# A hybrid decoder step: the sample's recurrent states updated pair by pair, the head norms' roots in two batches, and the sample's gates ordered behind a later tile

## The chip, the cores and the metric

The kernel runs on one core of a Trainium2 chip. The core has a matrix engine (PE, with its weight loads shown apart as PEld), a vector engine (DVE), a scalar engine (ACT), a general engine (POOL) and SP, whose queue issues the DMA transfers here. Each engine works through its own queue of instructions strictly in order; engines wait for each other by semaphores. The metric is the device time of one execution in microseconds, the median of several runs.

## The reference: what is computed

One inference step of a single decoder layer, over 2048 prompt positions and over 64 sample rows (8 sequences of 8 new positions each). Every row is normalised and goes through one input projection; its columns are split between two mixers and their gates:

```python
h = rmsnorm(x, norm_w)
z = h @ w_in
q, k, v, qb, kb, vb, g_lr, gate_a, gate_b = jnp.split(z, split_points(), axis=-1)
...
o_a = attend(q, k, v)
log_a = jax.nn.log_sigmoid((g_lr @ w_gate_up + b_gate).astype(jnp.float32)) / GATE_TAU
o_b, s_fin = gla_chunked(heads(qb, H_B) * (DK_B ** -0.5), heads(kb, H_B), heads(vb, H_B),
                         heads(log_a, H_B), s0)
o_b = rmsnorm(o_b, gla_norm_w)
mixed = jnp.concatenate(
    [o_a.reshape(B, L, D_A) * jax.nn.silu(gate_a.astype(jnp.float32)),
     o_b.reshape(B, L, D_B) * jax.nn.silu(gate_b.astype(jnp.float32))], axis=-1)
y = x + mixed.astype(x.dtype) @ w_out
```

Mixer A is a dilated sliding-window attention with 8 heads, a mixture of three branches. Mixer B is a gated linear attention with 4 heads, key width 64 and value width 128. It carries a state per sequence and head; a chunk ends with

```python
state = (jnp.exp(b_last)[..., None] * state
         + jnp.einsum('bhsk,bhsv->bhkv', kc * jnp.exp(b_last[:, :, None] - b), vc))
```

The output of each head of mixer B is normalised by the root of its mean square. The new states of the 8 sample sequences are outputs of their own.

## The kernel before

The 2048 prompt rows are 16 tiles of 128 (`NT`), the sample is one tile of 64 rows (`"s"`). The kernel goes through these stages: the projections q, k, v with the first two branches of the attention; the projection `qkb` with the third branch; the projections `g` and `vb`, and then `gb`, beside the linear attention; and the output stage, in which every tile's gated mixture is multiplied with `w_out`, beside the sample's attention over the cached keys and values. Intermediate results go through DRAM (`ob_d` holds mixer B's outputs, `ga_d` and `gb_d` the gates' inputs).

**What sets the order.** Stages are Python generators. `weave` traces several of them in turns: each has a number of expected turns, and the one with the smallest share done goes next; one that yields `WAIT` is passed over. This fixes the program's order. The framework then plans each engine's queue at compile time: a planner (`schedule_with_timeline_sim=True`) goes through the program with modelled durations, and takes an instruction for an idle engine among those that it holds to be ready. Buffers of a pool are reused under a tag (`bufs` of them), and memory of a closed pool is reused tile by tile; an instruction that needs a buffer waits for the last user of what lay there. With `tc.issue_after(x)`, instructions on the engine of `x` are queued behind `x`, without a semaphore.

**The stage around the change.** The last `weave` of the linear attention runs the projection `gb` (`rest("gb")`, 130 turns; PE lines L1137, evicted by ACT at L752), the prompt's recurrence (`gla_prompt`, weight 32), the sample's part (`sample_gla`, weight 32) and the loading of `w_out` in two halves (`load_w`, scaled and converted at L659 on ACT and L660 on DVE). It ends when the recurrence and the sample's part have ended; what is left of `gb` then runs on beside `first_mixes`, which prepares tiles 0 and 1 for the output stage.

The recurrence goes through 8 blocks of 256 rows. `gla_core.front` computes a decay on POOL (L237), its exponential on ACT (L243) and two products on DVE (L248, L251); `back` multiplies on PE (L287). `chunk` finishes 128 rows: the state's sum on DVE (L1307), the output stored to `ob_d`, and in `gla_out` each head's sum of squares (L344), which goes into four columns of `ob_ss`, 4(t+1) for tile t and 0 for the sample.

`sample_gla` first builds its operands like a block of the recurrence, in a tile `own` that has the tag `vx`. Then, for both pairs of heads `p`, it multiplies queries with the old states (L1434, `O_s`), and squares the outputs. In a second loop over the pairs, halves `q` of the 8 sequences and heads `j` of the pair, POOL makes a block `vx` (L1460: the values masked to four sequences, 64x512), PE multiplies it with the keys (L1466, `U_s`), POOL decays the old states (L1471), and DVE adds (L1477). There is one `vx` buffer, so each block waits for the matmul of the block before; each pair's states are stored by SP at L1482. The generator yields 21 times in all, 14 of them in these two loops.

When all this has been traced, `rsqrt` turns all 68 columns of `ob_ss` into `ob_rs` at once: a scale and shift on DVE (L122), logarithm and exponential on ACT (L123, L125), a correction in three steps on DVE (L138 to L140).

**The output stage.** `combine(t)` loads the three attention branches (`oc`), computes the gates, loads mixer B's outputs (`obl`) and scales them by `ob_rs` on ACT (L1607), weighs the branches (L1694 to L1717, L1702 being the weights and L1710 and L1716 partly on POOL) and leaves the mixture as two 16-bit parts `mt` (`parts_of`: ACT L1616, DVE L1617). `gates(t)` clamps the gate inputs on DVE (L1586), takes exponential, logarithm and exponential on ACT (L1588, L1589, L1590), multiplies and takes maxima on DVE (L1592). `turned` transposes `mt` on PE (L1626, `tm`) and evicts it on ACT (L1627, `mh`); `finish` multiplies with `w_out` (L1668). `first_mixes` does `combine(0)` and `combine(1)` and, when `gb` is done, transposes tile 0. `prompt_out` then goes through the tiles, mixing two tiles ahead; at t = 8 it also traces the sample's `gates` and `normed`, which the planner may place as early as their inputs allow.

## Time and profile before

| | |
|---|---|
| median of 3 runs | 1339.93 us (1339.32 to 1349.03) |
| profiled execution | 1338.29 us, span 1336.5 us |
| mean granted TensorE clock | 0.977 |
| PE busy | 1215.3 us, 91% of the span |
| DVE, ACT, POOL busy | 899.3, 849.7, 615.6 us |
| last state sum of the sample (L1477) | starts at 1068.23 us |
| end of the `gb` projection on PE | 1077.84 us |
| first transposition of the output stage (L1626) | 1085.85 us |

All times inside an execution are counted from the start of the profiled span. "Idle before, releaser" tells how long an engine waited before an instruction and whose end released it; "issue" is a wait for which the profile shows no releaser. The granted clock is the share of full speed at which the matrix engine was let run in a stretch.

### The profile page before, as it was taken

How to read it: one execution, taken by the hardware profiler on the slowest of the kernel's cores; microseconds unless marked ns; L12 is line 12 of the kernel's file. 1: busy time of each engine (PE TensorE's matmuls, PEld its weight loads, DVE VectorE, ACT ScalarE, POOL GpSimd, SP SyncE). 2: the span in 40 equal slices, each digit the busy share in tenths (PEclk: the TensorE clock that was granted, in tenths of full speed). 3: DMA queues.
4: the chain of work that ended last, by engine and by line, in shares of the span. 5: the costliest groups of instructions: out<-in, count | busy, mean ns of one | idle time of the engine just before them, and what ended most of it. 6: DMA issues, size and time to landing. Idle time of an engine off the chain costs nothing.

```text
span 1336.5 us, 27968 instructions
## 1 busy us (share of the span) xinstructions
PE 1215.3 (91%) x9754; PEld 726.4 (54%) x9754; DVE 899.3 (67%) x2317; ACT 849.7 (64%) x2281; POOL 615.6 (46%) x596
## 2 busy tenths in 40 slices
PE   3897999989899798998999999999999969999998
PEld 1343565555556555576777666667555435444443
DVE  6366767787777876776763888776552368887751
ACT  5655787777668875878995565455662466555520
POOL 0076554778678735661112856665342133332310
PEclk9899999999999999999999989999999989999999
DMA  7859866777966599958886647453452777998952
GB/s 256 249 160 247 224 189 151 212 208 218 223 179 190 173 268 270 323 186 203 211 193 196 219 155 207 148 168 100 128 196 89 249 250 270 376 323 323 330 205 78
DMA packets 251807, 285.39 MB, mean 214 GB/s; under 512 B 125441, under 2 KB 160338, under 8 KB 251666
## 3 DMA queue, kind: packets, MB, share of 16 engines
q1 hardware_dynamic: 251666, 283.60, 71.0%
q8 instruction: 77, 1.26, 0.4%
q14 instruction: 64, 0.52, 0.1%
HBM read 183.12 MB, written 75.24 MB: 193 GB/s over the span
## 4 chain that ended last, share of the span: by engine, by line
PE 42%; DVE 17%; DMA 13%; issue 12%; POOL 9%; ACT 5%; SPq 2%; POOLq 0%; DVEq 0%; ACTq 0%
PE acc_gb L1137 5%; PE Y L1668 4%; PE acc_vb L1137 4%; PE acc_qkb L1137 4%; PE acc_q L1137 3%; PE acc_g L1137 3%; PE t L472 3%; PE s L454 3%; PE O L487 3%; PE acc_v L1137 2%; POOL pr L975 2%; PE acc_k L1137 2%; DMA T_q<-qp_d 2%; DVE ks L248 2%; DVE qs L251 2%
## 5 line engine op out<-in xcount | busy, mean ns | idle before, releaser
L1137 PEld LDWEIGHTS <-hr 128*128 128x128 f16 x1824 | 173.8, 99 | 127.7 <-issue 12.1
L1137 PEld LDWEIGHTS <-hl 128*128 128x128 f16 x1248 | 122.5, 100 | 154.4 <-issue 28.5
L465 ACT ACTIVATE p<-p,o 128x256 f32<-128x256 f32 (+1 forms) x384 | 173.4, 455 | 47.3 <-DVE o L462 40.6
L1668 PE MATMUL Y<-w_o,mh 128*128 128x512 f16 x768 | 179.3, 383 | 4.2 <-ACT mh L1627 3.5
L975 POOL TENSOR_TENSOR pr<-k,qb 128x512 f32<-128x512 f32 x96 | 132.9, 1384 | 90.1 <-DVE sck L980 54.9
L439 POOL TENSOR_TENSOR pt<-p,pt 128x512 f16<-128x512 f32 (+1 forms) x80 | 93.9, 1175 | 154.6 <-ACT pt L438 134.2
L487 PE MATMUL O<-v,pt 128*128 128x128 f16 x1200 | 111.6, 222 | 21.1 <-POOL pt L439 9.4
L1668 PEld LDWEIGHTS <-mh 128*128 128x128 f16 x768 | 72.3, 98 | 91.0 <-issue 10.9
L980 DVE TENSOR_REDUCE sck<-pr 128x8 f32<-128x512 f32 x128 | 85.7, 680 | 48.5 <-POOL pr L975 48.3
L472 PE MATMUL t<-ident,p 128*128 128x128 f32 x600 | 108.1, 283 | 9.1 <-ACT p L465 4.1
L487 PEld LDWEIGHTS <-pt 128*128 128x128 f16 x1200 | 82.6, 99 | 46.5 <-POOL pt L439 14.3
L1710 POOL TENSOR_TENSOR tc<-oc,w 128x512 f32<-128x512 f32 x32 | 44.2, 1401 | 134.6 <-DVE w L1702 96.4
L1137 PE MATMUL acc_v<-w_v,hl 128*128 128x512 f16 x384 | 97.0, 397 | 8.2 <-DVE vp L769 3.1
L1137 PE MATMUL acc_g<-w_g,hr 128*128 128x272 f16 (+1 forms) x768 | 102.5, 282 | 0.0
L462 DVE CUSTOM_DVE_ANT_0 p<-s,m3w,scl_s 128x128 f32<-128x128 f32 (+1 forms) x256 | 89.1, 395 | 14.6 <-PE s L454 7.2
L1137 PE MATMUL acc_q<-w_q,hl 128*128 128x512 f16 x384 | 91.4, 386 | 6.0 <-ACT zs_k L687 5.3
L1137 PE MATMUL acc_k<-w_k,hl 128*128 128x512 f16 x384 | 91.2, 383 | 3.0 <-ACT zs_k L687 2.5
L1137 PE MATMUL acc_vb<-w_vb,hr 128*128 128x512 f16 x384 | 92.0, 379 | 0.0
L454 PE MATMUL s<-kk,qq 128*128 128x256 f16 (+1 forms) x512 | 81.5, 270 | 8.2 <-DMA kk<-kp_d 4.5
L237 POOL TENSOR_TENSOR D_e<-b_e 128x512 f32<-128x512 f32 x56 | 61.0, 1094 | 58.5 <-ACT E L243 45.6
L1137 PE MATMUL acc_gb<-w_gb,hr 128*128 128x512 f16 x384 | 87.9, 380 | 0.0
L243 ACT ACTIVATE E<-D_e 128x256 f32<-128x256 f32 x112 | 43.7, 417 | 60.8 <-DVE ks L248 34.6
(507 smaller groups left out, 2595.9 us busy)
## 6 DMA issues: line engine op xcount, KB each, us to landing
k<-in_cache_k_win SPq DMA_DIRECT2D x104, 256.0 KB
sv<-in_cache_v_win SPq DMA_DIRECT2D x24, 1024.0 KB
hr<-h_d SPq DMA_DIRECT2D x44, 512.0 KB
qb<-q_d SPq DMA_DIRECT2D x64, 256.0 KB
o_d<-o SPq DMA_DIRECT2D x96, 132.0 KB
oc<-o_d SPq DMA_DIRECT2D x48, 264.0 KB
x<-in_x_prompt SPq DMA_DIRECT2D x16, 512.0 KB
h_d<-hl SPq DMA_DIRECT2D x16, 512.0 KB
```

What stands on the lines that cost most here:

```text
L237: dec = POOL.tensor_tensor(dv, bv, bv[:, :, 0:1, B - 1 : B].to_broadcast([P, M, 2, B]), ALU.subtract)
L439: POOL.tensor_tensor(l, f, h, ALU.subtract)
L454: PE.matmul(s_ps[:, i * w : (i + 1) * w], q, k, start=(n == 0), stop=(n == len(prods) - 1),)
L462: DVE.tensor_tensor_reduce(s[:, sl], s_ps[:, sl], mask, neg, BIG, ALU.add, ALU.min, nmf(i))
L465: ACT.activation(s[:, sl], s[:, sl], AF.Exp, bias=nmf(i), scale=-1.0, accum_out=denf(i))
L472: PE.transpose(p_ps[:, i * P : (i + 1) * P], t["s"][:, i * P : (i + 1) * P], ident[:])
L487: PE.matmul(o_, t["pt"][:, c, (i * nb + b) * P : (i * nb + b + 1) * P], vf(i, b), start=(n == 0), stop=(n == 2 * nb - 1),)
L975: POOL.tensor_tensor(pr[:], kt, qt, ALU.mult)
L980: DVE.tensor_reduce(out, pr[:].rearrange("p (u k d) -> p u k d", u=2, k=4), AX.X, ALU.add)
L1137: PE.matmul(z, a_[:, k, :], w[:, p_, k, cols], start=(k == 0 and i == 0), stop=(k == KT - 1 and i == 2),)
L1668: PE.matmul(Y[:], a_[:, k, :], w_[:, part, k, :512], start=(i == 0), stop=(i == len(prods) - 1),)
L1710: eng.tensor_tensor(t_[:], oc[:, g, :, 0:64], w[:, g].unsqueeze(2).to_broadcast([P, NH, HD]), ALU.mult,)
```

## The change

Four edits, in the stages from 950 us on.

1. **Pair by pair.** `sample_gla` has one loop over the pairs of heads. A pair's four blocks `vx` are traced first, into four buffers (`own` takes one of the four before); then the pair's outputs, the decays of its old states, a yield, and for each half the two matmuls and the sum. The generator yields 17 times, 10 of them in this loop.
2. **Roots in two batches, in place.** `ob_ss` now holds tile t in columns 4t and the sample in the last four. `head_scales` takes the roots of 32 columns, tiles 0 to 7, when chunk 9 has been traced, and of the other 36 after the recurrence. The roots overwrite the sums, and `normed` reads them from `ob_ss`.
3. **Marks.** `parts_of` keeps the two instructions that write a tile's `mt`.
4. **Sample's gates.** The sample's `gates` and `normed` are traced under `issue_after` of tile 2's marks: their ACT instructions are queued behind L1616 of tile 2, their DVE instructions behind L1617 of tile 2. Their DMA issues on SP aren't bound.

```diff
@@ -1238,6 +1238,7 @@
         )
         gpools = (gl, gt, ps_O, ps_S, ps_P)
 
+        gc_pool = gc
         masks = gc.tile([P, len(LEVELS), 32], F32, name="gmask")
         scan_m = gc.tile([P, 256], F32, name="scan_m")
         wgu = gc.tile([17, 256], F32, name="wgu")
@@ -1272,8 +1273,11 @@
         POOL.memset(ob_ss[:], 1.0)
 
         def at_heads(t):
-            c = 0 if t == "s" else 4 * (t + 1)
+            c = 4 * (NT if t == "s" else t)
             return ob_ss[:, c : c + 4]
+
+        def head_scales(pool, c):
+            rsqrt(pool, ob_ss[:, c], ob_ss[:, c], 1.0 / 128.0, P, c.stop - c.start, f"ob{c.start}")
 
         def chunk(core, gc):
             c, r0 = gc % 2, gc * P
@@ -1311,6 +1315,8 @@
                     )
             gla_out(gt, O, P, r0, f"c{gc}", at_heads(gc))
             mixed.add(gc)
+            if gc == 9:
+                head_scales(gc_pool, slice(0, 32))
 
         vbs = {}
 
@@ -1386,7 +1392,7 @@
             yield from upto("vb", "s")
             vb = g1.tile([NS, 512], F32, name="vb_s")
             SP.dma_start(vb[:], vb_d[S : S + NS, :])
-            own = g1.tile([P, 512], F32, name="own", tag="vx")
+            own = g1.tile([P, 512], F32, name="own", tag="vx", bufs=4)
             DVE.memset(own[:], 0.0)
             E, ks, qs = (
                 own[:, 0:128].rearrange("p (i c) -> p i c", i=2), own[:, 128:256], own[:, 256:320]
@@ -1419,7 +1425,22 @@
             qe, eb, kdt, Am = core.qe, core.eb, core.kdt, core.Ac
             so = A["state_gla_sample"][0]
             ebv = eb[:].rearrange("p a (b t) -> p a b t", t=8)
+            blocks = {}
+
+            def block(p, q, j):
+                h = 2 * p + j
+                vx = blocks[p, q, j] = g1.tile([NS, 4, P], F32, name=f"vx_{h}_{q}", tag="vx", bufs=4)
+                POOL.tensor_tensor(
+                    vx[:],
+                    vb[:, h * P : (h + 1) * P].unsqueeze(1).to_broadcast([NS, 4, P]),
+                    bm[:, 4 * q : 4 * q + 4].unsqueeze(2).to_broadcast([NS, 4, P]),
+                    ALU.mult,
+                )
+
             for p in range(2):
+                for q in range(2):
+                    for j in range(2):
+                        block(p, q, j)
                 O = ps_O.tile([P, 512], F32, name=f"O_s{p}", tag="O")
                 for j in range(2):
                     h, js = 2 * p + j, slice(64 * j, 64 * j + 64)
@@ -1449,31 +1470,21 @@
                         jk[:NS], ob[:, j * P : (j + 1) * P], AF.Square,
                         accum_out=at_heads("s")[:NS, h : h + 1],
                     )
+                for q in range(2):
+                    sq = S0[p][:, 4 * q : 4 * q + 4, :]
+                    POOL.tensor_tensor(
+                        sq, sq, ebv[:, p, 4 * q : 4 * q + 4, 7:8].to_broadcast([P, 4, P]), ALU.mult
+                    )
                 yield
-            for p in range(2):
                 for q in range(2):
                     sq = S0[p][:, 4 * q : 4 * q + 4, :]
                     U = ps_O.tile([P, 512], F32, name=f"U_s{p}{q}", tag="O")
                     for j in range(2):
                         h = 2 * p + j
-                        vx = g1.tile([NS, 4, P], F32, name=f"vx_{h}_{q}", tag="vx")
-                        POOL.tensor_tensor(
-                            vx[:],
-                            vb[:, h * P : (h + 1) * P].unsqueeze(1).to_broadcast([NS, 4, P]),
-                            bm[:, 4 * q : 4 * q + 4].unsqueeze(2).to_broadcast([NS, 4, P]),
-                            ALU.mult,
+                        PE.matmul(
+                            U[64 * j : 64 * j + 64], kdt[:NS, 0, 64 * h : 64 * h + 64],
+                            blocks.pop((p, q, j))[:], start=True, stop=True,
                         )
-                        PE.matmul(
-                            U[64 * j : 64 * j + 64], kdt[:NS, 0, 64 * h : 64 * h + 64], vx[:],
-                            start=True, stop=True,
-                        )
-                        if j == 0:
-                            POOL.tensor_tensor(
-                                sq, sq,
-                                ebv[:, p, 4 * q : 4 * q + 4, 7:8].to_broadcast([P, 4, P]),
-                                ALU.mult,
-                            )
-                            yield
                     DVE.tensor_tensor(
                         sq, sq, U[:].rearrange("p (b v) -> p b v", b=4), ALU.add
                     )
@@ -1564,8 +1575,7 @@
         va = cb1.tile([P, 2], F32, name="va")
         for i, c_ in enumerate((2048.0 / M_SCALE, 1.0 / (P_SCALE * W_SCALE * H_SCALE * V_SCALE))):
             DVE.tensor_scalar(va[:, i : i + 1], powers["v"][:], c_, None, ALU.mult)
-        ob_rs = cb1.tile([P, 4 * (NT + 1)], F32, name="ob_rs")
-        rsqrt(cb1, ob_rs[:], ob_ss[:], 1.0 / 128.0, P, 4 * (NT + 1), "ob")
+        head_scales(cb1, slice(32, 4 * (NT + 1)))
 
         def scales(c):
 
@@ -1601,20 +1611,24 @@
             pool, tag = (cb1, "obs") if t == "s" else (cb, "ob")
             ob = pool.tile([P, 512], F32, name=f"obl_{t}", tag=tag)
             SP.dma_start(ob[:n], ob_d[rows, :])
-            c = 0 if t == "s" else 4 * (t + 1)
+            rs = at_heads(t)
             for h in range(4):
                 s = slice(h * P, (h + 1) * P)
-                ACT.activation(ob[:n, s], ob[:n, s], AF.Copy, scale=ob_rs[:n, c + h : c + h + 1])
+                ACT.activation(ob[:n, s], ob[:n, s], AF.Copy, scale=rs[:n, h : h + 1])
             return ob
 
         ident16 = cb1.tile([P, P], F16, name="ident16")
         DVE.tensor_copy(ident16[:], ident[:])
 
+        marks = {}
+
         def parts_of(tag, mix):
 
             mt = cb.tile([P, 2, D], F16, name=f"mt_{tag}", tag="mt")
-            ACT.activation(mt[:, 0], mix[:], AF.Copy)
-            DVE.tensor_tensor(mt[:, 1], mix[:], mt[:, 0], ALU.subtract)
+            marks[tag] = (
+                ACT.activation(mt[:, 0], mix[:], AF.Copy).ins,
+                DVE.tensor_tensor(mt[:, 1], mix[:], mt[:, 0], ALU.subtract).ins,
+            )
             return mt
 
         def turned(tag, mt):
@@ -1750,7 +1764,10 @@
                 rows = slice(t * P, (t + 1) * P)
                 if t == NT // 2:
                     at_s = slice(S, S + NS)
-                    mixes["s"] = gates("s", NS, at_s), normed("s", NS, at_s)
+                    with ExitStack() as order:
+                        for m_ in marks[2]:
+                            order.enter_context(tc.issue_after(m_))
+                        mixes["s"] = gates("s", NS, at_s), normed("s", NS, at_s)
                 if t == NT - 1:
                     while "attended" not in mixed:
                         yield WAIT
```

## The prediction

> **What bounds the kernel now.** I read the page's busy times first, then busy time by stretches of the span, then the waits around the one stretch that stands out, and last that stretch instruction by instruction.
>
> ```profile
> PE 1215.3 (91%) x9754; PEld 726.4 (54%) x9754; DVE 899.3 (67%) x2317; ACT 849.7 (64%) x2281; POOL 615.6 (46%) x596
> ```
>
> PE (TensorE) is busy for 91% of the span. The change touches the linear-attention stage and what follows it, from about 950 us on; there the stretches read (length, then PE, weight load, DVE, ACT, POOL busy, granted clock, DMA share, GB/s):
>
> ```profile
> 950.00:1000.00 50.00, 50.00 (x463) 27.78 (x462) 28.00 (x71) 37.96 (x109) 17.21 (x20) 1.00 0.48 164
> 1000.00:1050.00 50.00, 50.00 (x457) 28.29 (x456) 10.91 (x32) 16.29 (x58) 12.88 (x16) 1.00 0.41 125
> 1050.00:1100.00 50.00, 39.66 (x189) 16.93 (x187) 31.02 (x90) 27.43 (x50) 12.81 (x12) 0.90 0.78 258
> 1100.00:1150.00 50.00, 48.39 (x373) 24.54 (x372) 41.33 (x101) 30.53 (x50) 17.90 (x14) 1.00 0.88 314
> ```
>
> PE has no idle time at all from 950 to 1050, while the sample's states are updated: nothing that this update waits for costs time there. The hole is at the seam to the output stage, 10.3 us idle in 1050 to 1100, at a clock of 0.90. Cut finer:
>
> ```profile
> 1078.00:1086.00 8.00, 0.15 (x2) 0.15 (x3) 5.56 (x14) 7.72 (x16) 5.83 (x6) 0.80 0.59 177
> 1086.00:1088.00 2.00, 1.55 (x15) 1.29 (x14) 1.70 (x7) 1.08 (x2) 0.38 (x1) 0.50 0.94 250
> 1088.00:1090.00 2.00, 1.95 (x8) 0.61 (x5) 0.00 (x0) 0.12 (x1) 0.00 (x0) 0.58 1.14 229
> 1093.00:1095.00 2.00, 1.81 (x5) 0.71 (x6) 1.96 (x6) 2.00 (x4) 2.00 (x2) 0.53 1.02 406
> 1095.00:1096.50 1.50, 1.50 (x5) 0.47 (x4) 1.50 (x4) 0.39 (x1) 0.81 (x2) 0.50 1.03 407
> ```
>
> The idle 8 us are followed by two stretches at about half clock. Their PE work, 1.55 + 1.95 + 1.81 + 1.50 = 6.8 us, would take about 3.4 us at full clock, so the hole costs 3.4 us beside the idle time. The Trainium skill ("TensorE: Matmul & The Clock Gate", Part 1) states that after an idle window of about 3.4 us the clock is halved, until PE was busy for about as long; an estimate by it alone is one stretch of 3.4 us at half clock, 1.7 us lost. The trace shows two stretches, so I take its 3.4.
>
> The waits in 1045 to 1110 (total us, times, longest):
>
> ```profile
> POOL vx L1460 <- PE U_s L1466: 21.8, 3, 11.4
> PE tm L1626 <- ACT mt L1616: 8.0, 1, 8.0
> DVE zl_s L1586 <- DMA zl_s<-gb_d: 5.3, 1, 5.3
> ACT zgb L752 <- issue: 4.7, 1, 4.7
> PE Y L1668 <- ACT mh L1627: 0.8, 1, 0.8
> PE tm L1626 <- DVE mt L1617: 0.4, 1, 0.4
> SPq L1482 <- DVE S L1477: 6.6, 1, 6.6
> ```
>
> PE waits for `mt`, the first output tile's mixture. What sets that is seen in the order of time (start, length):
>
> ```profile
> 1056.38 0.69 DVE L1586 TENSOR_SCALAR zl<-zl 128x1024 f32<-128x1024 f32 x1
> 1060.71 5.00 ACT L659 ACTIVATE w_o<-wr_o,ns_o 128x512 f16<-128x512 f32 x8
> 1067.00 1.05 ACT L1588 ACTIVATE sa<-zl 128x1024 f32<-128x1024 f32 x1
> 1067.31 10.53 PE L1137 MATMUL acc_gb<-w_gb,hr 128*128 128x512 f16 x48
> 1068.23 0.68 DVE L1477 TENSOR_TENSOR S<-S,U_s 128x512 f32<-128x512 f32 x1
> 1069.23 0.19 DVE L122 TENSOR_SCALAR rv_ob<-ob_ss 128x68 f32<-128x68 f32 x1
> 1072.75 0.69 ACT L752 ACTIVATE zgb<-acc_gb,wi_gb 128x512 f32<-128x512 f32 x1 [4.70 <-issue]
> 1073.33 0.25 ACT L123 ACTIVATE rr_ob<-rv_ob 128x68 f32<-128x68 f32 x1
> 1073.48 1.13 ACT L1589 ACTIVATE sa<-sa,ones 128x1024 f32<-128x1024 f32 x1
> 1074.67 1.04 ACT L1590 ACTIVATE sa<-sa 128x1024 f32<-128x1024 f32 x1
> 1075.00 0.69 DVE L1586 TENSOR_SCALAR zl_s<-zl_s 64x1024 f32<-64x1024 f32 x1 [5.32 <-DMA zl_s<-gb_d]
> 1076.12 0.23 DVE L140 SCALAR_TENSOR_TENSOR ob_rs<-ra_ob,rr_ob 128x68 f32<-128x68 f32 x1
> 1076.26 0.68 DVE L1592 CUSTOM_DVE_ANT_0 zl<-zl,sa 128x512 f32<-128x512 f32 x1
> 1078.73 1.26 ACT L1607 ACTIVATE obl_s<-obl_s,ob_rs 64x128 f32<-64x128 f32 x4
> 1079.16 0.24 DVE L1702 SCALAR_TENSOR_TENSOR w<-w,smxa,mn 128x24 f32<-128x24 f32 x1
> 1084.74 1.06 ACT L1616 ACTIVATE mt<-mix 128x1024 f16<-128x1024 f32 x1
> 1085.85 1.03 PE L1626 MATMUL tm<-ident,mt 128*128 128x128 f16 x8 [8.01 <-ACT mt L1616]
> ```
>
> The last two `gb` tiles end at 1077.84 (1067.31 + 10.53), and nothing can follow before 1085.85. Two chains run to `mt`. The gates' chain had its input at 1057.07, started its exponential only at 1067.00 behind the eight `w_o` conversions, and stopped in the middle, because ACT's queue has next the eviction of a `gb` tile (L752). The profile names no releaser for its 4.70 us; half of the x48 row's matmuls, one tile, are done at 1072.6, so I put it down to them. The chain goes on at 1073.48. The roots' chain (L122 to L140) lies behind the last state sum on DVE, then behind the same eviction, then behind the sample's gates. Both end within half a microsecond at 1076.3.
>
> **The change, part by part.** *States pair by pair.* Work is neither added nor removed: eight blocks, four decays, sixteen matmuls, four sums. POOL's waits for PE (21.8 us in this window) go, as a block no longer needs the buffer of the block before. By themselves they are worth nothing, since PE was full. What moves is the end of the update: the last sum at 1068.23, SP's 6.6 us wait for it, and, in program order, the whole first mixture, because it is traced only when the sample's part has ended; that part takes 17 turns of the weave and not 21, each worth 130/32 turns of `gb`, so at most 16 turns, two tiles, 10.53 us by the x48 row. The recurrence also has to end, so I count on less.
>
> *Roots in two batches.* The six small instructions are issued twice: 0.19 to 0.25 us each, some 1.3 us on ACT and DVE in a stage where ACT idles 12 us of 50 (37.96 busy) and DVE 22; nothing on the path. Tile 0's scales then exist long before 1076. But with the gates' chain ending at the same moment, this alone saves under 1 us: L1590 ends at 1075.71, and L1592 could start then and not at 1076.26.
>
> *Sample's gates pinned.* On DVE 0.69 us and the 5.32 us wait at 1069.7 to 1075.0 leave the seam, on ACT the 1.26 us of `obl_s`. They land behind tile 2's mixture, where DVE has 8.7 us free of 50 (41.33 busy): nothing on PE's path. SP's loads aren't pinned, and stay ahead.
>
> *The sum.* The queues are written anew at compile time, so the new place of ACT's L1588 and L1589 isn't in this trace. Bounds: if they stay, the chain is 0.6 us shorter; if the exponential runs as soon as its input is there, 1067.00 - 1057.07 = 9.9 us. I take a value by the nearest row: behind the `w_o` conversions still, but not cut by the eviction, so that L1589 follows L1588 at 1068.05 and not 1073.48, 5.4 us earlier, and 0.6 us for the roots out of DVE's way, 6.0 in all. The first transposition then comes at 1079.85, 2.0 us after `gb`. A pause so much shorter than 8 us I take to leave the clock whole: 3.4 us. Together 9.4 us; the 0.8 and 0.4 us waits behind it stay. Given back: the output stage's loads, which share the DMA with the sample's values at over 1.0 in the fine rows, can't all start 9 us sooner, since their buffers come free with `gb`. Bounds 0 to 3 us, I take 1.4. Net 8.0 us. The profiled execution took 1338.3 us (span 1336.5), the median is 1.6 us above: 1338.3 - 8.0 + 1.6 = 1332 us.
>
> **Rivals.** *The order on ACT stays* (the exponential behind the conversions, the logarithm behind the eviction). For it: eviction and conversions are the same, and the roots weren't the only late chain. Against: the sample's part ends sooner, so tile 0 is planned sooner. 0.6 us saved and as much lost elsewhere: 1340, say 1336 to 1342.
>
> *Slower: the blocks come into the recurrence's way.* Pair 0's blocks can now be issued before the recurrence's last decays, and one of the four buffers belongs to `own`, which PE releases only around 998.8.
>
> ```profile
> 994.24 1.05 POOL L237 TENSOR_TENSOR D_e<-b_e 128x512 f32<-128x512 f32 x1 [1.13 <-ACT E L243]
> 998.85 1.03 POOL L1460 TENSOR_TENSOR vx<-vb_s,bm 64x512 f32<-64x512 f32 x1 [3.56 <-PE sc_smp L287]
> 994.35 1.02 DVE L248 TENSOR_TENSOR own<-kq_smp,own 128x64 f32<-128x64 f32 x1
> L248 DVE TENSOR_TENSOR own<-kq_smp,own x3: 223/526/1022, 965.4 to 994.3; 128x64 f32<-128x64 f32 x3
> ```
>
> Four blocks ahead of a decay on POOL cost the recurrence 4 x 1.03 = 4.1 us; and a DVE product that begins beside a POOL one lasts until that one ends: 1.02 us and not 0.22. Four such are 3.2 us more. With 7.3 us of slip and no gain at the seam that is 1340 + 7.3 = 1347, and 1351 if a decay also stands behind the 3.56 us wait for the held buffer; with the forecast's gain in, it decides only beyond 8 us of slip. The Trainium skill ("SBUF — State Buffer", Who interferes with whom) states that a GpSimd instruction and a VectorE one with two inputs in SBUF hold a shared port pair one at a time, the other blocked in full; by that rule, which the 1.02 us row bears out, moving blocks forward among DVE's products is a loss. Against it: PE's 50.00 of 50 hides a slip of the recurrence as long as `gb` tiles are left.
>
> *The whole seam closes*: 8.0 + 3.4 + 0.8 + 0.4 = 12.6 us, nothing given back: 1327, or 1325 with the output stage's own small waits.
>
> **Numbers.** Forecast (5 to 12 us gained, 1328 to 1335) 0.57; order stays 0.23; slower 0.11; whole seam 0.09. The range from 1325 to 1344 leaves out most of the slower rival and what lies past either end, under 2 in 10. A measurement of this kernel tells about 1%, 13.4 us: faster means under 1326.5, which needs the whole seam and more, 0.12; slower means above 1353.3, the far end of that rival and what I overlook, 0.05; the rest 0.83.
>
> **What would show it.** In the changed profile: `vx` without waits for `U_s`, the last `S` sum well before 1068; a root on 32 columns among the recurrence's instructions; no sample gates before tile 2's `mt`; L1589 directly behind L1588; `tm`'s wait for `mt` near 2 us and not 8; a clock of 1.00 right behind it; 1100 to 1300 unchanged in busy time. It is wrong if `tm` still waits 7 us or more, if the last chunk comes later than now, or if the wait returns as one for a load of the output stage.

## The result, and the profile after

The changed kernel takes 1333.22 us (median, 1325.97 to 1336.92), the kernel before, timed beside it, 1341.58 us (1338.57 to 1349.03). The ratio is 0.9927, with a 95% interval from 0.9908 to 0.9946: 8.4 us less, where 8 had been forecast. The profiled execution of the changed kernel took 1336.84 us (span 1335.0, mean granted clock 0.979), near the top of its own spread, and the one of before 1338.29, below all 16 of its timed runs. So the two profiles differ by 1.5 us only, and where the 8.4 us lie has to be read piece by piece, not from the spans.

The busy time of each engine after the change:

```profile
PE 1209.3 (91%) x9754; PEld 724.8 (54%) x9754; DVE 904.2 (68%) x2321; ACT 849.1 (64%) x2283; POOL 614.8 (46%) x596
```

PE has as many instructions as before, but 6.0 us less busy time (1215.3 then). Three of the four stretches of the prediction (length, then PE, weight load, DVE, ACT, POOL busy, granted clock, DMA share, GB/s):

```profile
950.00:1000.00 50.00, 48.38 (x461) 26.58 (x460) 32.46 (x72) 35.27 (x100) 20.31 (x24) 1.00 0.41 127
...
1050.00:1100.00 50.00, 46.06 (x232) 21.77 (x231) 34.05 (x92) 30.79 (x63) 13.74 (x12) 0.93 0.81 272
1100.00:1150.00 50.00, 47.50 (x375) 23.91 (x374) 39.23 (x107) 31.14 (x52) 16.56 (x14) 1.00 0.92 330
```

The hole from 1050 to 1100 has shrunk: 46.06 us busy and not 39.66, at a clock of 0.93 and not 0.90. Two things are worse: 1.6 us of idle time are new in 950 to 1000, and 1100 to 1150 has 47.50 busy and not 48.39. The seam itself in the order of time (start, length; in brackets the idle time before, and what ended it):

```profile
1060.27 1.04 ACT L1598 ACTIVATE sa<-zl 128x1024 f32<-128x1024 f32 x1
1062.66 1.14 ACT L1599 ACTIVATE sa<-sa,ones 128x1024 f32<-128x1024 f32 x1
1068.21 5.00 ACT L659 ACTIVATE w_o<-wr_o,ns_o 128x512 f16<-128x512 f32 x8
1078.25 1.06 ACT L1629 ACTIVATE mt<-mix 128x1024 f16<-128x1024 f32 x1 [1.32 <-DVE mix L1731]
1080.85 0.61 PE L1640 MATMUL tm<-ident,mt 128*128 128x128 f16 x8
1081.75 0.62 PE L1640 MATMUL tm<-ident,mt 128*128 128x128 f16 x8 [0.29 <-DVE mt L1630]
1082.38 1.06 ACT L1598 ACTIVATE sa<-zl 128x1024 f32<-128x1024 f32 x1 [2.39 <-DVE zl L1596]
1083.34 0.67 ACT L752 ACTIVATE zgb<-acc_gb,wi_gb 128x512 f32<-128x512 f32 x1
1083.91 1.14 ACT L1599 ACTIVATE sa<-sa,ones 128x1024 f32<-128x1024 f32 x1
1084.95 1.92 ACT L1641 ACTIVATE mh<-tm 128x1024 f16<-128x1024 f16 x2
1086.02 6.26 PE L1682 MATMUL Y<-w_o,mh 128*128 128x512 f16 x15 [3.65 <-ACT mh L1641]
```

(In the changed kernel L1598 and L1599 are the gates' exponential and logarithm, L1629 writes `mt`, L1640 transposes it, L1641 evicts `mh`, L1682 multiplies.) The exponential of tile 0's gates starts at 1060.27, before the eight `w_o` conversions. So `mt` is there 2.6 us before `gb` ends, and the first transposition follows `gb` with no wait. The 8.0 us wait for `mt` is gone. A new one stands two steps on: `mh`, the eviction of the transposed tile, is next on ACT only at 1084.95, behind the exponential of tile 2's gates, which waits 2.39 us for DVE, then a `gb` eviction, then tile 2's logarithm. PE waits 3.65 us for it, and the clock goes down:

```profile
1086.00:1088.00 2.00, 1.98 (x5) 0.72 (x6) 1.12 (x1) 2.00 (x4) 1.31 (x2) 0.50 0.51 147
1088.00:1090.00 2.00, 2.00 (x6) 0.73 (x5) 1.44 (x4) 1.69 (x5) 2.00 (x4) 0.50 0.80 237
1090.00:1093.00 3.00, 3.00 (x12) 1.09 (x10) 2.93 (x10) 0.34 (x1) 1.36 (x3) 0.70 0.90 221
```

About 5.8 us run at half clock (4 us at 0.50, and 1.8 of the last 3 for a mean of 0.70), so 2.9 us are lost to it; before it was 3.4.

Ahead of the seam the update of the states looks different too. In the trace of before, one call of `U_s` (two records) takes 1.0 us until PE's next work begins; after the change the two calls of a half stand side by side, four records, and take 1.0 us together. PE in order, before:

```profile
1066.30 1.07 PE L1466 MATMUL U_s<-vx,kdt_smp 64*64 64x512 f32 x2
1067.31 10.53 PE L1137 MATMUL acc_gb<-w_gb,hr 128*128 128x512 f16 x48
```

and after:

```profile
1019.01 1.06 PE L1484 MATMUL U_s<-vx,kdt_smp 64*64 64x512 f32 x4
1020.01 2.76 PE L1137 MATMUL acc_gb<-w_gb,hr 128*128 128x512 f16 x12
```

All four halves are so paired; in three of them other small matmuls fall between the first record and the rest. The last state sum now starts at 1039.18 us, where it started at 1068.23. The whole stretch of `gb`, from its first matmul for the prompt (L1137) to its last, shortens (before, then after):

```profile
947.90:1077.90 130.00, 129.94 (x1050) 69.06 (x1048) 54.05 (x149) 69.23 (x199) 33.21 (x39) 1.00 0.49 163
```

```profile
953.80:1081.00 127.20, 125.58 (x1053) 68.94 (x1052) 63.02 (x169) 75.37 (x211) 36.05 (x41) 1.00 0.55 177
```

4.3 us less PE work and, because of the new 1.6 us wait, 2.7 us less time (the windows shown are widened to 0.1 us). That wait is the recurrence's, in the answer on PE's waits in this stretch (total us, times, longest):

```profile
PE O L1298 <- DVE Sbd L1311: 1.6, 1, 1.6
```

It stands in the four profiles that have both pair by pair and the roots, and in no other. In the changed kernel POOL is making blocks `vx` (948.70 to 951.73) when a DVE product of the recurrence starts; with pair by pair alone the same product comes after the blocks (first row after, second row pair by pair alone):

```profile
950.92 2.12 DVE L248 TENSOR_TENSOR ks<-kq_e,E 128x256 f32<-128x256 f32 x1
```

```profile
947.22 0.43 DVE L248 TENSOR_TENSOR ks<-kq_e,E 128x256 f32<-128x256 f32 x1 [3.10 <-PE sc_e L270]
```

The product takes 1.7 us longer. That this makes the wait is read from the order of the instructions; no run tests it alone.

Behind the seam, from 1098 on, PE's largest waits were, before and after:

```profile
PE Y L1668 <- ACT mh L1627: 2.8, 2, 2.4
PE OS L1897 <- DMA sv<-in_cache_v_win: 1.6, 2, 0.9
```

```profile
PE R L1848 <- DVE k1T L355: 2.9, 1, 2.9
PE OS L1914 <- DMA sv<-in_cache_v_win: 2.5, 2, 1.6
```

To add the pieces up, each execution is cut at three points: the output of chunk 7 (the eighth `ob_c` eviction on ACT, 887.52 before and 893.61 after), the first of these `gb` matmuls, and the last. Up to chunk 7's output no edit has an instruction of its own, and PE, ACT, DVE and POOL have the same instructions in the same order in all the kernels; yet that point lay between 885.2 and 894.1 us in the eleven executions profiled for this case, and two of the kernel before alone differ by 6.1 us. What lies ahead of it is spread from one execution to the next. Behind it (us, worked out from each profile, differences in the text taken before rounding; "20 us" is the stretch right behind `gb`):

```
                  chunk 7   gb     PE busy  gb end  PE busy  clock  PE idle   gb end   chunk 7
                  to gb     length in gb    to Y    in 20 us there  later     to end   to end
before            60.4      129.9  129.9    10.3     9.7     0.74   11.7      258.7    449.0
before, again     60.4      129.9  129.9    10.1     9.7     0.74   11.5      258.2    448.5
after             60.2      127.2  125.6     5.0    16.1     0.83   13.7      254.0    441.4
after, again      60.2      127.2  125.6     5.4    15.6     0.83   14.1      256.5    443.9
pair by pair      60.4      125.3  125.3     6.4    14.7     0.83   12.8      256.0    441.7
roots             57.5      130.1  130.1     2.4    15.2     0.83   15.0      258.0    445.6
pin               60.4      129.9  129.9    11.9    10.6     0.74   13.3      259.9    450.3
neighbours        60.4      127.3  127.3     8.0    13.9     0.83   15.2      258.7    446.4
pair + roots      57.5      127.2  125.6     6.5    15.0     0.83   13.5      255.1    439.7
roots + neighb.   57.5      127.4  127.4     5.8    15.7     0.83   13.4      252.4    437.4
mh first          58.5      127.2  125.6     1.7    17.0     1.00   14.0      251.3    437.0
```

From before to after: 0.2 us ahead of `gb`, 2.7 in it, 4.6 behind it, together 7.6. In the second pair of profiles it is 4.6 (448.5 to 443.9), with 1.7 behind `gb`. The medians say 8.4.

### The profile page after: what moved, and what is told of

Its sections match the earlier page's. It is cut to its first block, busy times and chain, and to the rows that moved or that the text cites. A ratio compares the mean times of both kernels' runs of the same rounds, so it can differ in the third digit from the quotient of the medians.

```text
span 1335.0 us, 27979 instructions
## 1 busy us (share of the span) xinstructions
PE 1209.3 (91%) x9754; PEld 724.8 (54%) x9754; DVE 904.2 (68%) x2321; ACT 849.1 (64%) x2283; POOL 614.8 (46%) x596
## 4 chain that ended last, share of the span: by engine, by line
PE 37%; DVE 19%; DMA 14%; issue 11%; POOL 9%; ACT 6%; SPq 2%; POOLq 0%; DVEq 0%; ACTq 0%
PE Y L1682 4%; PE acc_vb L1137 4%; PE acc_gb L1137 4%; PE acc_g L1137 3%; POOL pr L975 3%; DMA T_q<-qp_d 3%; PE acc_qkb L1137 3%; DMA qb<-q_d 2%; PE O L487 2%; PE t L472 2%; PE s L454 2%; PE acc_q L1137 2%; DVE p L462 2%; DVE qs L251 2%; POOL pt L439 2%
## 5 line engine op out<-in xcount | busy, mean ns | idle before, releaser
L1137 PEld LDWEIGHTS <-hr 128*128 128x128 f16 x1824 | 173.8, 98 | 125.8 <-issue 9.8
L1137 PEld LDWEIGHTS <-hl 128*128 128x128 f16 x1248 | 122.3, 100 | 152.7 <-issue 26.1
L1682 PE MATMUL Y<-w_o,mh 128*128 128x512 f16 x768 | 178.8, 386 | 5.2 <-ACT mh L1641 3.6
L1682 PEld LDWEIGHTS <-mh 128*128 128x128 f16 x768 | 73.3, 99 | 95.8 <-issue 14.8
L1137 PE MATMUL acc_v<-w_v,hl 128*128 128x512 f16 x384 | 94.4, 389 | 7.9 <-DVE vp L769 2.5
L1137 PE MATMUL acc_g<-w_g,hr 128*128 128x272 f16 (+1 forms) x768 | 101.3, 279 | 0.0
L462 DVE CUSTOM_DVE_ANT_0 p<-s,m3w,scl_s 128x128 f32<-128x128 f32 (+1 forms) x256 | 89.0, 395 | 13.7 <-PE s L454 6.2
L1137 PE MATMUL acc_q<-w_q,hl 128*128 128x512 f16 x384 | 92.4, 389 | 3.7 <-ACT zs_k L687 2.4
L1137 PE MATMUL acc_k<-w_k,hl 128*128 128x512 f16 x384 | 89.9, 379 | 4.4 <-ACT zs_k L687 2.9
L1137 PE MATMUL acc_vb<-w_vb,hr 128*128 128x512 f16 x384 | 93.2, 384 | 0.0
L454 PE MATMUL s<-kk,qq 128*128 128x256 f16 (+1 forms) x512 | 82.6, 273 | 11.7 <-DMA kk<-kp_d 7.3
L237 POOL TENSOR_TENSOR D_e<-b_e 128x512 f32<-128x512 f32 x56 | 60.9, 1094 | 57.9 <-ACT E L243 38.3
L1137 PE MATMUL acc_gb<-w_gb,hr 128*128 128x512 f16 x384 | 87.0, 379 | 0.0
## 6 DMA issues: line engine op xcount, KB each, us to landing
k<-in_cache_k_win SPq DMA_DIRECT2D x104, 256.0 KB
qb<-q_d SPq DMA_DIRECT2D x64, 256.0 KB
```

What stands on the lines that cost most here:

```text
L237: dec = POOL.tensor_tensor(dv, bv, bv[:, :, 0:1, B - 1 : B].to_broadcast([P, M, 2, B]), ALU.subtract)
L454: PE.matmul(s_ps[:, i * w : (i + 1) * w], q, k, start=(n == 0), stop=(n == len(prods) - 1),)
L462: DVE.tensor_tensor_reduce(s[:, sl], s_ps[:, sl], mask, neg, BIG, ALU.add, ALU.min, nmf(i))
L1137: PE.matmul(z, a_[:, k, :], w[:, p_, k, cols], start=(k == 0 and i == 0), stop=(k == KT - 1 and i == 2),)
L1682: PE.matmul(Y[:], a_[:, k, :], w_[:, part, k, :512], start=(i == 0), stop=(i == len(prods) - 1),)
```

## The experiments

Each kernel is the kernel before with one or two edits, unless another is named. The table above has a line for each.

**Pair by pair alone.** The first edit without the others:

```diff
-            own = g1.tile([P, 512], F32, name="own", tag="vx")
+            own = g1.tile([P, 512], F32, name="own", tag="vx", bufs=4)
...
+                for q in range(2):
+                    for j in range(2):
+                        block(p, q, j)
...
-            for p in range(2):
```

> Only the pair-by-pair edit with its four buffers; roots in one batch, sample's gates unpinned. Theory 1 (two separate shares: the two U_s matmuls of a half, now neighbours on PE, run side by side and save about 4 us of PE time; and the seam gets shorter because the first tile's gates no longer stand behind the w_o conversions on ACT, about 5 us): a_only brings both, 8 to 9 us less than before, ratio 0.993 to 0.994, U_s four at a time in about 1.06 us, first Y about 5 us after the end of gb and not 10. Rival (the roots' batch frees the seam, the pairs only tidy up the order): the seam stays at 8 us of wait, at most 4 us less, ratio 0.997 or above.

Measured: 1333.92 us against 1341.21, ratio 0.9949 (0.9926 to 0.9971). This edit has most of the gain, 7.3 us where 8 to 9 had been expected. The stretch of `gb` has 125.3 us of PE work in 125.3 us, and the seam's first wait is gone without the roots' batch:

```profile
1075.26 0.61 PE L1631 MATMUL tm<-ident,mt 128*128 128x128 f16 x8
1079.43 0.62 PE L1631 MATMUL tm<-ident,mt 128*128 128x128 f16 x8 [3.56 <-DVE mt L1622]
1081.84 9.78 PE L1673 MATMUL Y<-w_o,mh 128*128 128x512 f16 x31 [1.79 <-ACT mh L1632]
```

Here another step is late: the second part of `mt`, on DVE. The first transposition comes directly behind `gb`, but `Y` is 6.4 us behind it. So at the seam 3.9 us of pause went (10.3 to 6.4), and from the stretch of `gb` 4.6 us (129.9 to 125.3). From the end of `gb` to the end of the span only 2.7 of the 3.9 are left (258.7 to 256.0).

**Roots alone.** The second edit without the others:

```diff
+            if gc == 9:
+                head_scales(gc_pool, slice(0, 32))
...
-        ob_rs = cb1.tile([P, 4 * (NT + 1)], F32, name="ob_rs")
-        rsqrt(cb1, ob_rs[:], ob_ss[:], 1.0 / 128.0, P, 4 * (NT + 1), "ob")
+        head_scales(cb1, slice(32, 4 * (NT + 1)))
```

> Only the roots in two batches. Theory 1: the U_s matmuls stay apart (8 groups of about 1.07 us), the gates' exponential starts as soon as its input is there, as in the changed kernel, so the seam's share alone comes: about 5 us less, ratio 0.996. Rival (only the earlier end of the sample's states moves the gates): no change, ratio 0.999 to 1.001, tm still waits about 8 us for mt.

Measured: 1337.28 us, ratio 0.9973 (0.9960 to 0.9986), 3.9 us less. The prediction gave it less than 1 us. The stretch of `gb` is as long as before, with the `U_s` calls apart. The seam is short, and still the clock goes:

```profile
1080.35 0.62 PE L1631 MATMUL tm<-ident,mt 128*128 128x128 f16 x8 [0.64 <-ACT mt L1621]
1082.09 1.04 PE L1673 MATMUL Y<-w_o,mh 128*128 128x512 f16 x4 [1.12 <-ACT mh L1632]
1084.80 0.71 PE L1631 MATMUL tm<-ident,mt 128*128 128x128 f16 x8 [1.67 <-DVE mt L1622]
1086.89 7.22 PE L1673 MATMUL Y<-w_o,mh 128*128 128x512 f16 x21 [1.39 <-ACT mh L1632]
```

```profile
1083.00:1085.00 2.00, 0.33 (x5) 0.20 (x5) 2.00 (x5) 1.28 (x2) 0.00 (x0) 1.00 0.87 257
1085.00:1087.00 2.00, 0.61 (x9) 0.36 (x7) 1.97 (x9) 2.00 (x3) 0.49 (x1) 0.55 0.74 178
1087.00:1089.00 2.00, 2.00 (x5) 0.62 (x5) 1.34 (x4) 0.78 (x1) 2.00 (x2) 0.50 0.89 215
```

No wait is longer than 1.67 us, but from 1083 to 1087 PE works 0.94 us of 4, and then the clock is 0.50 to about 1092. From the end of `gb` to the end of the span the kernel takes 258.0 us, 0.4 less than the mean of before: the time won at the seam returns, in part as a longer wait of PE for the sample's values in the output stage:

```profile
PE OS L1902 <- DMA sv<-in_cache_v_win: 5.6, 2, 4.8
```

Before, that wait was 1.6 us. The clock also falls there, to 0.51 from 1133 to 1140 us, and once more to 0.53 from 1214.8 to 1218.4, together some 3.4 us; in the trace of before it has a mean of 1.00 from 1097.8 to the end. So neither expectation held: the seam's pause is shorter, and the end doesn't move with it. What is won lies ahead of `gb`: 57.5 us from chunk 7's output to the first `gb` matmul instead of 60.4. There PE waited before, and with the roots' batch (the second row), for one step of the recurrence:

```profile
PE U L1286 <- DVE kdt_e L336: 3.0, 2, 1.7
```

```profile
PE U L1290 <- DVE kdt_e L336: 0.6, 1, 0.6
```

The batch brings its six instructions into the middle of the recurrence, and the order of DVE's queue around them comes out another way. The copy `kdt_e`, for which PE waited twice, now comes earlier. Nothing in the edit aims at this, and the changed kernel, which has this batch too, gets only 0.2 us of it (60.2); the open point at the end shows where the two part. The batch itself is not cheap there, in the changed kernel:

```profile
900.33 1.24 DVE L138 TENSOR_TENSOR ra_ob<-rr_ob 128x32 f32<-128x32 f32 x1
903.93 1.05 DVE L140 SCALAR_TENSOR_TENSOR ob_ss<-ra_ob,rr_ob 128x32 f32<-128x32 f32 x1
```

The two-input steps L138 and L140 take 1.24 and 1.05 us on 32 columns, where L140 took 0.23 us on 68 columns in the trace of before. POOL works on products of its own at that time. This agrees with the rule of the Trainium skill ("SBUF — State Buffer", Who interferes with whom) that the prediction weighed.

**The pin alone.** The marks and the sample's gates behind tile 2's `mt`:

```diff
+                    with ExitStack() as order:
+                        for m_ in marks[2]:
+                            order.enter_context(tc.issue_after(m_))
-                    mixes["s"] = gates("s", NS, at_s), normed("s", NS, at_s)
+                        mixes["s"] = gates("s", NS, at_s), normed("s", NS, at_s)
```

> Only the sample's gates pinned behind tile 2's mixture. Theory 1 and the prediction: under 1 us, ratio 0.999 to 1.001; tm still waits 7 to 8 us for mt, as ACT still holds the logarithm behind the eviction. Rival (the 5.3 us in which DVE waited for the sample's gates were the cause): 4 to 5 us less, ratio 0.996 to 0.997.

Measured: 1341.69 us, ratio 1.0008 (0.9992 to 1.0023). The sample's gates leave the seam, and the seam stays:

```profile
1092.64 1.03 PE L1630 MATMUL tm<-ident,mt 128*128 128x128 f16 x8 [8.25 <-ACT mt L1619]
```

**Neighbours alone.** The kernel before with two `vx` buffers: both blocks of a half are made first, then its two `U_s` calls are issued one behind the other. The second loop over the pairs, its yields and everything else stay.

```diff
-                        PE.matmul(
-                            U[64 * j : 64 * j + 64], kdt[:NS, 0, 64 * h : 64 * h + 64], vx[:],
-                            start=True, stop=True,
-                        )
...
+                    for j in range(2):
+                        h = 2 * p + j
+                        PE.matmul(
+                            U[64 * j : 64 * j + 64], kdt[:NS, 0, 64 * h : 64 * h + 64], vxs[j][:],
+                            start=True, stop=True,
+                        )
```

> The kernel before with one thing changed: two vx buffers, a half's two blocks made first, then its two U_s matmuls next to each other; still a second loop, with as many yields. Theory 1: three of the four halves have their matmuls as neighbours, so PE saves about 3 us in the gb stretch (U_s four in 1.06 us), and part of the seam comes with it as the states end about 5 us sooner: 3 to 7 us less, ratio 0.995 to 0.998. Rival (the time in which four U_s overlap is only how their ends are modelled in the trace): gb from its first to its last matmul takes as long as before, 129.6 us, and nothing is gained but what the seam gives.

Measured: 1338.24 us, ratio 0.9978 (0.9964 to 0.9992), 3.0 us less. Three of the four halves came out as neighbours, the fourth did not:

```profile
1035.17 1.07 PE L1477 MATMUL U_s<-vx,kdt_smp 64*64 64x512 f32 x4
1036.18 3.63 PE L1137 MATMUL acc_gb<-w_gb,hr 128*128 128x512 f16 x16
...
1054.12 1.07 PE L1477 MATMUL U_s<-vx,kdt_smp 64*64 64x512 f32 x2
```

The stretch of `gb` has 127.23 us of PE work, 2.7 less than the 129.94 of before, and is 2.7 us shorter. The same matmuls cost 0.9 us less for each pair that stands together. So the rival is refuted: the stretch itself is shorter, and not only the modelled ends. Behind `gb` nothing is won, 258.7 us as before, although `Y` comes 2.3 us earlier. At 0.9 us the four pairs of the changed kernel account for 3.6 of its 4.3 us less PE work; no run separates the rest. The two calls read the same 64 rows and write the two halves of one accumulator. The Trainium skill ("TensorEngine Tiling (Array Packing)", Key Properties) states that matmuls on different tiles of the array can run in parallel; the rows agree for such calls as long as they are neighbours in PE's queue.

**After, again.** The changed kernel on the chip of the three runs below:

> The changed kernel once more, beside the others on one chip. Both theories: ratio 0.990 to 0.995 as before; its profile has the gb stretch near 127 us, Y waiting 3 to 4 us for mh, and half clock behind that.

Measured: 1332.38 us against 1341.54, ratio 0.9937 (0.9916 to 0.9959). The seam is the same, with 3.67 us of waiting for `mh`. From the end of `gb` to the end of the span it takes 256.5 us, where the first profile had 254.0: so much may differ from one execution to the next. Some 1.7 us of it is a stretch at a clock of 0.55, from 1272.0 to 1275.8, that the first profile doesn't have.

**`mh` first.** The changed kernel, with tile 2's mixture ordered behind tile 0's second eviction `mh`, so that neither tile 2's exponential nor its logarithm can stand ahead of it on ACT:

```diff
-                ACT.activation(mhl[:, a], pt[:], AF.Copy)
+                marks["mh", tag] = ACT.activation(mhl[:, a], pt[:], AF.Copy).ins
...
-                        mixes[t + 2] = combine(t + 2)
+                        with ExitStack() as order:
+                            if t == 0:
+                                order.enter_context(tc.issue_after(marks["mh", 0]))
+                            mixes[t + 2] = combine(t + 2)
```

> The changed kernel, with ACT's work on tile 2 queued behind the eviction of tile 0's transposition (mh), so that neither tile 2's exponential, which waits for DVE, nor the logarithm stands before it. Theory 2 (what is left of the seam is ACT's order: 3.65 us of wait, and about 3 us more because that wait is long enough to halve the clock for 35 matmuls): Y starts 1 to 2 us after tm, no stretch at half clock behind it, 4 to 6 us less than the changed kernel. Rival (the output stage is paced by its loads, so what is gained at the seam is waited for later, at sv or at the values' loads): Y starts earlier, but the end moves by less than 2 us against the changed kernel.

Measured: 1326.94 us (1324.66 to 1330.98), ratio 0.9900 (0.9874 to 0.9925), 5.4 us below the changed kernel on the same chip, the lowest median of this study. `Y` starts 1.7 us behind `gb`, and the clock stays whole:

```profile
1073.65 1.06 PE L1640 MATMUL tm<-ident,mt 128*128 128x128 f16 x16
1075.56 7.99 PE L1682 MATMUL Y<-w_o,mh 128*128 128x512 f16 x36 [0.85 <-ACT mh L1641]
```

```profile
1075.00:1077.00 2.00, 1.44 (x7) 0.60 (x8) 1.55 (x4) 2.00 (x3) 1.06 (x1) 1.00 0.11 37
```

So the eviction that stood behind tile 2's gates was what was left of the seam. From the end of `gb` to the end of the span this kernel takes 251.3 us, the changed kernel 254.0 and 256.5: 2.7 to 5.2 us less by these single profiles, which is what going without the pause and the half clock is worth at the end. Another 1.7 us lies ahead of `gb` (58.5 against 60.2), where this edit does nothing; the open point below is about that.

**Pair by pair and roots, no pin.** The changed kernel without its third and fourth edits:

> Pair by pair and roots in two batches, without the pin of the sample's gates. Theory 1: the seam's share comes once, by either edit, and the pairs' share of 4.4 us once, so it stands with the changed kernel: ratio 0.990 to 0.995, within 1.5 us of it; mh is evicted behind obl_s and the eviction of gb, about 1 us later. Rival (the pin matters once the other two are in): 3 us or more slower than the changed kernel.

Measured: 1333.35 us, ratio 0.9935 (0.9910 to 0.9960), the same as with the pin. The late step is again the second part of `mt` (3.66 us), then `mh`, for which `Y` waits 1.38 us:

```profile
1079.76 1.03 PE L1636 MATMUL tm<-ident,mt 128*128 128x128 f16 x8 [3.66 <-DVE mt L1627]
```

The pin moves the wait by one step, from `mt` to `mh`, and the medians show no gain from it (1332.38 with it).

**Roots and neighbours.** The second edit together with the neighbours of above, without the loop pair by pair:

> Roots in two batches, and of the pairs' edit only that a half's two U_s matmuls stand next to each other (two buffers, second loop kept). Theory 1: the shares add up: gb stretch 2.7 us shorter than with the roots alone, as in the kernel with neighbours alone, and the seam as with the roots alone; 3.6 + 2.7 = about 6 us less than before, ratio 0.994 to 0.997. Rival (both act on the seam only): no better than either alone, ratio 0.997 to 0.998.

Measured: 1329.80 us (1323.75 to 1333.13), ratio 0.9910 (0.9879 to 0.9941), 11.7 us less than before. About 6 had been expected. In its profile 3.0 us lie ahead of `gb` (57.5 against 60.4), 2.4 in it and 6.0 behind it (252.4 against a mean of 258.4), 11.4 in all. The first two are those of the kernels with one of the edits; the 6.0 are not, since each of these has 0.4 or less behind `gb`. After the first 20 us behind `gb` this profile has a mean clock of 1.00 to the end, and PE waits 3.2 us for the sample's values, where the roots alone had two stretches near half clock and 5.6 us. It is one profile, of the second fastest of six runs, so whether the kernel or the execution makes the 6.0 us stays open. The interval overlaps that of the changed kernel.

**Before, again**, for one more profile of the kernel before:

> The kernel before once more, for a second profile. If the edits act only from the gb projection on, what differs between executions of one kernel must lie ahead of it: gb starts anywhere between 943 and 955 us, as over the profiles so far, but gb takes 129.9 to 130.1 us of PE time again, Y starts 10 to 12 us after it, and from the end of gb to the end of the span it is 257 to 261 us. Rival (the profiles differ there as much as the kernels do): gb or the time behind it moves by 4 us or more.

Measured: 1343.95 us. Chunk 7's output comes at 893.65 and not 887.52. Behind it the execution takes 448.5 us, and the first took 449.0.

## Why the prediction came out

The number was right, 1332 for 1333.2, and half of its working was not: that the sum met the median is partly luck. By its own steps:

- *"By themselves they are worth nothing, since PE was full."* This step failed. That PE was full ruled out a gain from shorter waits; it did not rule out a gain from shorter PE time. Pair by pair, the two `U_s` calls of a half become neighbours and take 1.0 us together instead of each. The stretch of `gb` lost 4.3 us of PE work, and 2.7 us of its length, since 1.6 came back as a wait. The run with neighbours alone shows this for three pairs, without any other edit: 2.7 us.
- *"At most 16 turns, two tiles, 10.53 us"* of earlier tracing, of which the sum counted on less, with the exponential still behind the `w_o` conversions (5.4 us) and the roots out of the way (0.6). The mechanism was right, its size was at the other bound: the exponential started as soon as its input was there (clamped at 1060.00, started at 1060.27), as the 9.9 us bound had it.
- *The remaining wait near 2 us, the clock whole.* This step failed: the sum followed `mt` alone and took the 0.8 us wait for `mh` as it was. `tm`'s wait fell to 0.29 us, and `mh` waited behind tile 2's gates, 3.65 us. The clock was halved again, for 2.9 us lost instead of none. `Y` comes 5.0 us behind `gb` and not 10.3. The Trainium skill's window of about 3.4 us ("TensorE: Matmul & The Clock Gate", Part 1) agrees with 3.65 and with 0.85 us, and not with the run of the roots alone, where no wait was over 1.67.
- *Given back, 1.4 us.* Once the first 20 us behind `gb` are over, PE idles 13.7 us and not 11.7: 2.0 us, and 2.6 in the second pair of profiles. The sum left out the clock: behind a wait of 2.9 us for `k1T` it is 0.57 from 1211 to 1215 us, some 1.7 us more.
- *Net 8.0 us, all of it at the seam.* Behind `gb` it is 4.6 us in one pair of profiles and 1.7 in the other; 2.7 are in the stretch of `gb`. Two misses, one high and one low, made the sum right by luck.
- *Roots alone "under 1 us".* It measured 3.9, of which 3.0 lie in the recurrence ahead of `gb`, where the prediction looked for nothing. It counted on six instructions of 0.19 to 0.25 us; two of them took 1.24 and 1.05 us.
- *The pinned gates: nothing on the path.* Right as far as the medians tell: 1.0008 alone, and 1333.35 without it against 1332.38 with it.
- *Rival "the order on ACT stays"*: refuted, in the changed kernel the exponential stands ahead of the conversions. *"Slower"*: refuted. The last chunk's output comes 157.4 us behind chunk 7's (893.61 to 1051.0), and came 160.2 us behind it before (887.52 to 1047.7). Its mechanism is there on a small scale: the 1.6 us wait for `Sbd`, behind a DVE product that takes 2.12 us beside POOL's blocks.
- *"The whole seam closes", 1327*: not this change. The kernel with `mh` first closes the seam to 1.7 us and takes 1326.9, but with the gain of the neighbours in it.

What stays open: behind chunk 7's output the two profiles of the changed kernel are 7.6 and 4.6 us below those of before, and the medians 8.4 and 9.2. In both profiles the clock fell for a few microseconds around 912, behind a wait of 1.67 us for `kdt_e`:

```profile
910.00:912.00 2.00, 1.93 (x12) 1.13 (x13) 2.00 (x5) 0.42 (x1) 2.00 (x2) 0.73 0.00 0
912.00:914.00 2.00, 2.00 (x6) 0.61 (x5) 1.80 (x5) 0.42 (x1) 1.13 (x2) 0.50 0.00 0
```

The kernel with `mh` first has the same wait there (1.7 us) at a clock of 1.00, and is 1.7 us shorter in that stretch (58.5 against 60.2). The Trainium skill ("TensorE: Matmul & The Clock Gate", Part 1) states that the window is free-running. That the same pause then halves the clock in one execution and not in another would fit, but no run shows it.

Without the pin the wait is only 0.6 us and the stretch 57.5, although from chunk 7's output to `gb` PE, ACT, DVE and POOL have the same instructions in the same order as in the changed kernel. The two part at one DVE product, which starts 11.30 us behind chunk 7's output in both (first row the changed kernel, second the one without the pin):

```profile
904.91 1.31 DVE L248 TENSOR_TENSOR ks<-kq_e,E 128x256 f32<-128x256 f32 x1
```

```profile
902.27 0.41 DVE L248 TENSOR_TENSOR ks<-kq_e,E 128x256 f32<-128x256 f32 x1
```

POOL's decay (L237) starts with it, within 0.02 us. In the first it takes 1.04 us and the product is the one held up; in the second it takes 1.32 us, and the product is through at once. `kdt_e` then starts 1.1 us later in the first. The three profiles of kernels with roots and pin have the long product, the three with roots and no pin the short one. What decides it, and how often each outcome comes, is open; if some executions of the changed kernel have the short one, they are up to 2.7 us shorter, which would close part of the gap.

## What to carry to other kernels

A full engine rules out that shorter waits help, not that shorter work does: look whether small matmuls that write different halves of one accumulator stand side by side in PE's queue, since two such calls cost 1.0 us here when neighbours and 2.0 when apart. When a stall's last wait goes, follow the chain to the multiplication that ends it: the eviction two steps on stood behind a later tile's gates, and with it ordered first the median was another 5.4 us lower, of which 2.7 to 5.2 us lie behind `gb` in the profiles. Where a planner writes the queues, an edit's gain can lie where nothing was edited, so cut the executions at a point that no edit reaches and compare stretch by stretch.

## What was not expected of the hardware

- Two 64x64 by 64x512 `f32` calls on the two halves of one accumulator take 1.0 us together as neighbours (1019.01 to 1020.01), and 1.0 us each when other matmuls stand between (1066.30 to 1067.31).
- The granted clock fell to 0.50 behind one pause of 3.65 us, and also where no pause was over 1.67 us but PE was busy for only 0.94 of 4 us; with one pause of 0.85 us it stayed at 1.00. One wait of 1.67 us in the recurrence had both outcomes, in two kernels with the same wait.
- From one execution to the next, the time to chunk 7's output varied from 885.2 to 894.1 us. Between two profiles of the kernel before, 6.1 us of 887 lay there, and 0.5 of the 449 behind it.
- One DVE product of 128x256 took 1.31 us in three profiles and 0.41 in three others, with the same instruction order up to it and with POOL's product starting within 0.02 us of it.
